# A two-layer decoder trunk on one core: gate loads issued before the end of the u loop, evened gathers, gate preparation in two pieces, the last tile of v in halves

## The chip, the core and the metric

The kernel runs on one core of a Trainium2 chip. The metric is the device time of one execution in microseconds (us), as the median of several runs. The core has a matrix engine (PE, with PEld for its weight loads), a vector engine (DVE), an activation engine (ACT), a general engine (POOL, which here issues indirect gathers) and a sequencer (SP, which here issues most loads). Each engine works through its own instructions in the order in which the program has them, and waits on semaphores for the others. DMA transfers are issued by SP, ACT or POOL into a queue of that engine and move the data on 16 DMA engines.

## The reference

A mixer (layer 1: gated linear attention, layer 2: stick-breaking attention, both with memory attention), a residual LayerNorm, a PEER expert layer and another LayerNorm, twice, over 512 tokens of width 1024. The change lies in PEER, which is computed once in each layer:

```
q = (xf @ w_q).reshape(N, PEER_HEADS, 2, PEER_QHALF)
s = jnp.einsum('nhpd,hpkd->nhpk', q, subkeys)
top_s, top_i = lax.top_k(s, PEER_TOPK)
cand_s = top_s[:, :, 0, :, None] + top_s[:, :, 1, None, :]
cand_i = top_i[:, :, 0, :, None] * PEER_KEYS + top_i[:, :, 1, None, :]
best_s, best_pos = lax.top_k(cand_s, PEER_TOPK)
idx = jnp.take_along_axis(cand_i, best_pos, axis=-1)
g = jax.nn.softmax(best_s, axis=-1)
act = jax.nn.gelu(jnp.einsum('nd,nhkd->nhk', xt, u_tab[it]), approximate=False)
return jnp.einsum('nhk,nhkd->nd', gt * act, v_tab[it])
```

Each token has 8 heads, and each head picks 16 of 16384 experts (128 x 128 pairs of keys): rows of two tables, u and v, with 16384 rows of 1024 floats. A token's output is the sum over its 128 experts of gate times gelu(u row . x) times v row.

## The kernel before

**Two ways for the tokens.** 384 of the 512 tokens (three token tiles of 128) take the dense way: the product of all 16384 u rows with the tokens on PE, a gelu, a multiplication with a dense matrix of gates that is zero where an expert wasn't picked, and the product with all 16384 v rows on PE. The first token tile, tile 0, takes the sparse way: POOL gathers its 128 rows per token of u, and then of v, from memory (L1103), and DVE multiplies and adds them up (L1156 for u, L1175 for v). The first 16 tokens of the dense tiles ("side" tokens) have their gelu through gathers as well, so that the u products are 368 tokens wide and the v weights 384. Each number is split into a high and a low half (`split`, L97 on ACT makes the high half, L98 on DVE the low one), and a product is three matmuls: high by high, high by low, low by high.

**The stages of `peer`.** First comes the query phase (17 rows). Then the u loop runs over 128 blocks of 128 experts: block b multiplies u's block (L117, L118, L119 into `ph`) and in the next iteration takes the gelu (L1626) of block b − 1. For blocks 0 to 111 it is written to memory (`Ad`); for the last 16 (`KEEP`) it stays in the tile `keep`. Beside that, small pieces of work are handed out by generators, a budget in ns per block: `lead` and `work` select the experts and prepare the gates of the three dense tiles, `gst` makes the dense gates from one-hot matrices (L1446 on PE, `ob` on DVE, `obl` on ACT) and writes them to memory (`Gd`, issued on ACT's queue, L1516), and `gus` issues the gathers and the work on them. `GU`, `GU2` and `GU3` are the budgets of the gathers, `GR` that of the gates, `VS` the first v block that hands out gather work, and `VE` the number of blocks that the rate `vb` keeps free at v's end.

**The v loop** runs over 128 blocks too, and starts with the 16 kept blocks. `vprep(i)` loads v's block (`vr`), loads the gates of a group of blocks (`gl`; the first 6 blocks' go to `g0`, a part of the tile of `keep`) and multiplies gates by activations into the weights `w` (L1700 on DVE for 368 columns, L1702 on ACT for the 16 side tokens), splits v (`vh`, `vl`) and w (`whi` L1704 on ACT, `wlo` L1705 on DVE). It runs two blocks ahead of the matmuls. Blocks 0 to 122 add into all three token tiles (L285, L287, L289 into `acc`), 18 matmuls a block. The last 5 (`TAIL`) are kept back and then multiplied token tile by token tile, 30 matmuls each, so that a tile's LayerNorm (L984 to L1001) runs while PE works on the next tile. The LayerNorm of tile 0 comes from the sum of the gathers (`va`) and ends the `gus` stream.

**What sets the order.** The u loop stands in a part of the program whose order a scheduler works out, and so do the first instructions of v on SP and POOL. The v loop is in a `manual_schedule` for DVE, ACT and PE: there each of them runs its instructions in the order in which the code emits them. SP's order is that of the loads as they are issued. `load_raw` has the raw tiles of u and v on SP's queue. `preload(1)` and `preload(2)` issue gate loads on ACT's queue.

## Time and profile before

| | us |
|---|---|
| median of 3 runs | 2862.17 |
| lowest, highest | 2860.47, 2863.76 |
| profiled execution | 2858.78 |
| its span in the trace | 2857.1 |
| v matmuls, idle before L285 | 4.5 |
| gathers on POOL, busy (u and v) | 392.8 and 311.8 |

A row of the costliest groups gives line, engine, operation, output and inputs, the count, the busy time, the mean of one in ns, and the idle time before with what ended it. Rows of a timeline give the start, the duration and, in brackets, the idle time before the instruction and what ended it; "SPq" and "ACTq" are the time that an engine's sequencer spent on issuing a DMA. Busy times of matmuls overlap, since they are pipelined; a window's row gives the merged busy time. The mean clock of PE over the span was 0.998 of full speed.

### The profile page before, as it was taken

What the parts mean: (1) busy time and instruction counts of PE and PEld (TensorE: products, weight loads), DVE (VectorE), ACT (ScalarE), POOL (GpSimd) and SP (SyncE); (2) the same over time, 40 slices, a digit from 0 to 9 for tenths busy, and PEclk for the clock granted to TensorE, in tenths of its full rate; (3) what the DMA queues carried; (4) which work ended last, traced back from release to release, by engine and by line L of the source; (5) the groups of instructions that cost most, each with busy time, mean ns of one, the idle gap of its engine ahead of it and who ended that gap; (6) DMA issues with size and microseconds to landing.
All of it is one profiled execution on the core that took longest, in us unless ns stands there. A gap on an engine that the chain in (4) does not pass through costs nothing. (4 is left out here: it accounts for less than half of the span.)

```text
span 2857.1 us, 44575 instructions
## 1 busy us (share of the span) xinstructions
PE 2829.1 (99%) x16144; PEld 2507.4 (88%) x16144; DVE 2410.4 (84%) x4944; ACT 1445.3 (51%) x2723; POOL 778.2 (27%) x584
## 2 busy tenths in 40 slices
PE   9999999999999999999999999999999999999998
PEld 7888899999998888888877789999999988888886
DVE  5567999999877888888868779999998778888888
ACT  6342446757674333433446424477676744334333
POOL 0100253333333333333000002433333333234330
PEclk9999999999999999999999999999999999999999
DMA  5332589989999999999521325989999999999994
GB/s 194 103 112 67 176 313 321 343 316 342 340 344 369 338 371 370 373 380 365 195 81 52 111 82 202 327 319 325 327 343 342 340 368 336 373 375 371 368 359 165
DMA packets 311070, 806.87 MB, mean 282 GB/s; under 512 B 32176, under 2 KB 124480, under 8 KB 304448
## 3 DMA queue, kind: packets, MB, share of 16 engines
q1 hardware_dynamic: 195936, 414.93, 42.0%
q0 software_dynamic: 78336, 285.25, 27.6%
q10 hardware_dynamic: 36576, 103.85, 9.5%
q8 instruction: 126, 2.06, 0.3%
q14 instruction: 96, 0.79, 0.1%
HBM read 708.19 MB, written 94.68 MB: 281 GB/s over the span
## 5 line engine op out<-in xcount | busy, mean ns | idle before, releaser
L117 PE MATMUL ph<-xhi,uh 128*128 128x368 f32 x2048 | 687.7, 336 | 0.0
L119 PE MATMUL ph<-xhi,ul 128*128 128x368 f32 x2048 | 674.0, 329 | 1.2 <-DVE ul L98 1.2
L118 PE MATMUL ph<-xlo,uh 128*128 128x368 f32 x2048 | 673.4, 329 | 0.0
L1103 POOL DMA_INDIRECT gr<-in_un,gidx x256 | 392.8, 1534 | 796.9 <-DVE gr L1156 595.3
L97 ACT ACTIVATE vh<-vr 128x1024 fp32r<-128x1024 f32 x256 | 271.3, 1060 | 497.7 <-PE acc L289 445.2
L1103 POOL DMA_INDIRECT gr<-in_vt,gidx x256 | 311.8, 1218 | 646.9 <-DVE va L1175 553.4
L285 PE MATMUL acc<-vh,whi 128*128 128x512 f32 x1536 | 474.5, 390 | 4.5 <-ACT whi L1704 4.5
L287 PE MATMUL acc<-vl,whi 128*128 128x512 f32 x1536 | 474.2, 390 | 0.2
L289 PE MATMUL acc<-vh,wlo 128*128 128x512 f32 x1536 | 473.6, 389 | 0.0
L98 DVE TENSOR_TENSOR vl<-vr,vh 128x1024 fp32r<-128x1024 f32 x256 | 313.5, 1225 | 160.1 <-ACT vh L97 156.6
L97 ACT ACTIVATE uh<-ur 128x1024 fp32r<-128x1024 f32 x288 | 304.1, 1056 | 197.9 <-PE ph L118 174.3
L119 PEld LDWEIGHTS ph<-xhi,ul 128*128 128x128 f32 x2048 | 384.7, 188 | 2.2 <-DVE ul L98 2.2
L118 PEld LDWEIGHTS ph<-xlo,uh 128*128 128x128 f32 x2048 | 385.4, 188 | 0.0
L117 PEld LDWEIGHTS ph<-xhi,uh 128*128 128x128 f32 x2048 | 385.1, 188 | 0.1
L98 DVE TENSOR_TENSOR ul<-ur,uh 128x1024 fp32r<-128x1024 f32 x288 | 351.1, 1220 | 34.3 <-ACT uh L97 34.3
L285 PEld LDWEIGHTS acc<-vh,whi 128*128 128x128 f32 x1536 | 287.9, 188 | 66.4 <-ACT whi L1704 7.0
L287 PEld LDWEIGHTS acc<-vl,whi 128*128 128x128 f32 x1536 | 288.3, 188 | 61.7 <-DVE vl L98 2.2
L289 PEld LDWEIGHTS acc<-vh,wlo 128*128 128x128 f32 x1536 | 288.2, 188 | 60.8 <-DVE wlo L1705 1.0
L1156 DVE SCALAR_TENSOR_TENSOR gr<-gr,xnat 128x1024 f32<-128x1024 f32 x256 | 310.3, 1218 | 24.5 <-DMA gr<-in_un,gidx 24.5
L1175 DVE SCALAR_TENSOR_TENSOR va<-gr,gw,va 128x1024 f32<-128x1024 f32 x254 | 325.2, 1281 | 1.0
L1491 ACT ACTIVATE obl<-ob,rat 128x128 f16<-128x128 f16 x736 | 234.1, 392 | 38.0 <-DVE ob L1468 18.3
L1704 ACT ACTIVATE whi<-w 128x384 fp32r<-128x384 f32 x256 | 131.1, 512 | 78.5 <-DVE w L1700 78.1
(358 smaller groups left out, 4091.4 us busy)
## 6 DMA issues: line engine op xcount, KB each, us to landing
ur<-in_ut SPq DMA_DIRECT2D x256, 512.0 KB
vr<-in_vt SPq DMA_DIRECT2D x256, 512.0 KB
Gd<-gt ACTq DMA_DIRECT2D x48, 1024.0 KB
Ad<-act ACTq DMA_DIRECT2D x112, 368.0 KB
al<-Ad SPq DMA_DIRECT2D x112, 368.0 KB
gl<-Gd SPq DMA_DIRECT2D x26, 1536.0 KB
ur<-in_wq SPq DMA_DIRECT2D x32, 512.0 KB
bs<-in_b_st SPq DMA_DIRECT2D x14, 512.0 KB
```

The lines of the kernel that those rows point to most:

```text
L97: nc.scalar.activation(hi, raw, AF.Copy)
L98: sub = lambda: eng.tensor_sub(lo, raw, hi.bitcast(F32))
L117: nc.tensor.matmul(ps, h, xhi[:, c, sl], start=(c == 0), stop=False)
L118: nc.tensor.matmul(ps, h, xlo[:, c, sl], start=False, stop=False)
L119: nc.tensor.matmul(ps, l, xhi[:, c, sl], start=False, stop=(c == NC - 1))
L285: nc.tensor.matmul(acc[hf], lh, hi[:, hf * 512:(hf + 1) * 512], start=first, stop=False)
L287: nc.tensor.matmul(acc[hf], lh, lo[:, hf * 512:(hf + 1) * 512], start=False, stop=False)
L289: nc.tensor.matmul(acc[hf], ll, hi[:, hf * 512:(hf + 1) * 512], start=False, stop=last)
L1103: nc.gpsimd.indirect_dma_start(out=gr, out_offset=None, in_=tab, in_offset=bass.IndirectOffsetOnAxis(ap=idx[:, k:k + 1], axis=0))
L1156: nc.vector.scalar_tensor_tensor(gr, gr, 1.0, xr, op0=ALU.mult, op1=ALU.mult, accum_out=dst[:, k:k + 1])
L1175: nc.vector.scalar_tensor_tensor(va, gr, gw[:, k:k + 1], va, op0=ALU.mult, op1=ALU.add)
L1491: nc.scalar.activation(obl[:, q], ob[:, q, 0], AF.Copy, scale=rat[:, n0 + q:n0 + q + 1])
```

## The change

Six edits go together. (1) `VS` goes from 3 to 6 and `VE` from 8 to 6, `GU2` from 1350 to 1420, `GU3` goes, and `GR2` = 1.6 is the gates' budget once `work` is empty: gathers and gates are handed out at other rates. (2) `gate_prep` yields after its first half. (3) The body of the u loop becomes the function `ublock`, which runs for blocks 0 to 117 as before; then the remaining `work` and `gst` are emptied, the pools of that stage are given back, and blocks 118 to 128 run at the head of v's hand-ordered part. (4) The first two gate loads are issued there, behind blocks 119 and 121, on SP's queue; the second goes to a new tile "vt". (5) That tile holds the high and low halves of v's last two blocks later. (6) The last token tile of the tail does one half of its columns for all five blocks, and then the other.

```
@@ -1034,16 +1034,17 @@
 GU = 1230
 LOG = 0
 PF = 3
-VS = 3
+VS = 6
 GD = 1
 G0 = 6
-VE = 8
-GU2 = 1350
-GU3 = 1900
+VE = 6
+GU2 = 1420
 WF = 6100
 ER = 6
 GQ = 900
 GR = 1.25
+GR2 = 1.6
+BX = 118
 LEAD = 3
 TAIL = 5
 RB = 4
@@ -1347,12 +1348,13 @@
                         nc.scalar.activation(iT.rearrange("p n k r -> p r k n")[:, k], pt[:, 0:2 * P].rearrange("p (k n) -> p k n", k=2), AF.Copy)
                         nc.vector.tensor_copy(gT[:, :, k], h16)
                     nc.vector.tensor_copy(ghi, h16)
+                    yield 1000
                     nc.vector.scalar_tensor_tensor(glo, gp_, GS, h16, op0=ALU.mult, op1=ALU.subtract)
                     nc.vector.tensor_scalar(rat, ghi, 1e-30, None, op0=ALU.max)
                     nc.vector.reciprocal(rat, rat)
                     nc.vector.tensor_mul(rat, rat, glo)
                     ready.append((self.t, rat, iT, gT))
-                    yield 2500
+                    yield 1900
 
                     if self.t * P == T0:
                         nc.vector.tensor_copy(siT, iT[:, :SD])
@@ -1608,7 +1610,10 @@
             gst = Stream(gates(list(range(SD, P, OT))), side_gates(), gates(2 * list(range(0, P, OT))))
             lead.c = -2000.0
             ab, ph, later = None, None, []
-            for b in range(P + 1):
+            big = keep = g0 = None
+
+            def ublock(b):
+                nonlocal ab, ph, big, keep, g0
                 if b == KB:
                     big = gp.tile([P, 16 * NT * P], F32, tag="big", name="keep")
                     keep = big[:, :KEEP * TU].rearrange("p (b n) -> p b n", n=TU)
@@ -1616,6 +1621,7 @@
                 if 0 < b <= KB:
                     if (b - 1) % AB == 0:
                         ab = wk.tile([P, AB, TU], F32, tag="act", name="act")
+                pn = None
                 if b < P:
                     if b > 0:
                         prep(b + 18, later)
@@ -1629,7 +1635,7 @@
                     if (b - 1) % AB == AB - 1:
                         nc.scalar.dma_start(Ad[(b - 1) // AB], ab)
                 ph = pn
-                gst(GR)
+                gst(GR if work.q else GR2)
                 while later:
                     later.pop(0)()
                 if lead.q:
@@ -1637,9 +1643,12 @@
                 else:
                     work(WB if ready else WB0)
                 if b < P - 1:
-                    gus(GU if work.q else GU2 if b < KB else GU3)
+                    gus(GU if work.q else GU2)
                 if LOG:
                     print("block", b, len(work.q), len(gst.q), len(gus.q), gcount)
+
+            for b in range(BX):
+                ublock(b)
             work.drain()
             gst.drain()
 
@@ -1652,7 +1661,6 @@
                     sl = slice(hf * 512, (hf + 1) * 512)
                     nc.sync.dma_start(out_dram[t * P:(t + 1) * P, sl], E.x[:, t, sl])
 
-        acc = [[psum(E, name=f"acc{t}_{h}") for h in range(2)] for t in range(ND)]
         vp = {}
 
         gcuts = [0, G0] + list(range(KEEP, P + 1, GB))
@@ -1664,12 +1672,16 @@
         def load_gates(eng, dst, b, b1):
             eng.dma_start(dst, Gd[:, :, b:b1].rearrange("s p i n -> p s i n"))
 
-        pre = {}
+        pre = {0: g0}
 
         def preload(k):
             i, i1 = gcuts[k:k + 2]
-            pre[i] = new_gates(i, i1)
-            load_gates(nc.scalar, pre[i], vorder[i], vorder[i] + i1 - i)
+            if k == 1:
+                pre[i] = wv.tile([P, 4 * D], F32, tag="vt", name="gl", bufs=1)[:, :NSUB * (i1 - i) * TS].rearrange(
+                    "p (s i n) -> p s i n", s=NSUB, n=TS)
+            elif k > 1:
+                pre[i] = new_gates(i, i1)
+            load_gates(nc.scalar if k > 1 else nc.sync, pre[i], vorder[i], vorder[i] + i1 - i)
 
         def vprep(i):
             if i >= P:
@@ -1678,10 +1690,7 @@
             raw = load_raw(E, vt[b * P:(b + 1) * P], "vr")
             if i in gcuts:
                 g1 = gcuts[gcuts.index(i) + 1]
-                if i == 0:
-                    vp["g"] = g0
-                    load_gates(nc.sync, g0, b, b + g1)
-                elif i in pre:
+                if i in pre:
                     vp["g"] = pre.pop(i)
                 else:
                     vp["g"] = new_gates(i, g1)
@@ -1700,18 +1709,24 @@
             nc.vector.tensor_mul(w[:, SD:].rearrange("p (s n) -> p s n", n=TS), vp["g"][:, SD // TS:, i - vp["i"]],
                                  av.rearrange("p (s n) -> p s n", n=TS))
             nc.scalar.activation(w[:, :SD].rearrange("p (s n) -> p s n", n=TS), vp["g"][:, :SD // TS, i - vp["i"]], AF.Copy)
-            hi, lo = split(E, raw, "v", wv if i >= P - (TAIL - 3) else None)
+            if i == P - (TAIL - 3):
+                vp["t"] = wv.tile([P, 4, D], F32R, tag="vt", name="vtail", bufs=1)
+                vp["n"] = iter(range(4))
+            hi, lo = split(E, raw, "v", (lambda name: vp["t"][:, next(vp["n"])]) if i >= P - (TAIL - 3) else None)
             nc.scalar.activation(whi, w, AF.Copy)
             nc.vector.tensor_sub(wlo, w, whi.bitcast(F32))
             vp[i] = (whi, wlo, hi, lo)
 
         tail = []
         with tc.manual_schedule(engines={mybir.EngineType.DVE, mybir.EngineType.Activation, mybir.EngineType.PE}):
+            for b in range(BX, P + 1):
+                ublock(b)
+                if b in (BX + 1, BX + 3):
+                    preload((b - BX) // 2)
+            acc = [[psum(E, name=f"acc{t}_{h}") for h in range(2)] for t in range(ND)]
             vb = 1200 * (2 * P + SD - gcount[0] + PF) / (P - VE - VS)
             vprep(0)
             vprep(1)
-
-            preload(1)
             for b in range(P):
                 vprep(b + 2)
                 if b == 1:
@@ -1743,8 +1758,16 @@
         with tc.manual_schedule(engines={eng.PE} if last else {eng.PE, eng.DVE}):
             for t in range(ND):
                 sl = slice(t * P, (t + 1) * P)
-                for k, (whi, wlo, hi, lo) in enumerate(tail):
-                    mov_mm(E, acc[t], whi[:, sl], wlo[:, sl], hi, lo, False, k == TAIL - 1)
+                if t < ND - 1:
+                    for k, (whi, wlo, hi, lo) in enumerate(tail):
+                        mov_mm(E, acc[t], whi[:, sl], wlo[:, sl], hi, lo, False, k == TAIL - 1)
+                else:
+                    for hf in range(2):
+                        hs = slice(hf * 512, (hf + 1) * 512)
+                        for k, (whi, wlo, hi, lo) in enumerate(tail):
+                            nc.tensor.matmul(acc[t][hf], whi[:, sl], hi[:, hs], start=False, stop=False)
+                            nc.tensor.matmul(acc[t][hf], whi[:, sl], lo[:, hs], start=False, stop=False)
+                            nc.tensor.matmul(acc[t][hf], wlo[:, sl], hi[:, hs], start=False, stop=k == TAIL - 1)
                 if last:
                     finish(t + 1, acc[t])
                 elif t < ND - 1:
```

In the lists that follow, a row is one instruction or a run of equal ones ("x4"), in the order of its engine, without times. Line numbers in the rows of the changed kernel are its own, up to 12 higher than before.

On DVE, the end of v in layer 0: `w`, `vl` and `wlo` are the three steps of one v block (vtail is vl of the last two), `lny` from `va` begins the LayerNorm of tile 0. Before, the part from the last use of the gathers:

```order
L1175 SCALAR_TENSOR_TENSOR va<-gr,gw,va 128x1024
L1700 TENSOR_TENSOR w<-gl,al 128x368
L98 TENSOR_TENSOR vl<-vr,vh 128x1024
L1705 TENSOR_TENSOR wlo<-w,whi 128x384
L984 SCALAR_TENSOR_TENSOR lny<-xnat,va 128x512
L985 BN_STATS lnst<-lny 128x6
```

That wlo is block 119's. After the LayerNorm's last row (L1001), w, vl and wlo follow eight times, for blocks 120 to 127. In the changed kernel, from that last row on:

```order
L1001 SCALAR_TENSOR_TENSOR xnat<-lny,lnsm,bet 128x512 x2
L1709 TENSOR_TENSOR w<-gl,al 128x368
L98 TENSOR_TENSOR vl<-vr,vh 128x1024
L1717 TENSOR_TENSOR wlo<-w,whi 128x384
L1709 TENSOR_TENSOR w<-gl,al 128x368
L98 TENSOR_TENSOR vtail<-vr,vtail 128x1024
L1717 TENSOR_TENSOR wlo<-w,whi 128x384
L1709 TENSOR_TENSOR w<-gl,al 128x368
L98 TENSOR_TENSOR vtail<-vr,vtail 128x1024
L1717 TENSOR_TENSOR wlo<-w,whi 128x384
L984 SCALAR_TENSOR_TENSOR lny<-xnat,acc_0_10222 128x512
```

The LayerNorm of tile 0 has moved from behind block 119 to behind block 124: three blocks (125 to 127) follow it, and then the LayerNorm of the tail's first tile.

On ACT, the turn from u to v in layer 0: `uh` is the high half of u's block 127, `keep<-ph` a gelu, `w<-keep`, `vh` and `whi` the three steps of one v block. Before:

```order
L97 ACTIVATE uh<-ur 128x1024
L1626 ACTIVATE keep<-ph 128x368
L1702 ACTIVATE w<-keep 128x16
L1626 ACTIVATE keep<-ph 128x368
L97 ACTIVATE vh<-vr 128x1024
L1704 ACTIVATE whi<-w 128x384
L1702 ACTIVATE w<-keep 128x16
L97 ACTIVATE vh<-vr 128x1024
L1626 ACTIVATE keep<-ph 128x368
L1704 ACTIVATE whi<-w 128x384
L1665 DMA gl<-Gd 128x24x160
L1626 ACTIVATE keep<-ph 128x368
```

In the changed kernel:

```order
L97 ACTIVATE uh<-ur 128x1024
L1632 ACTIVATE keep<-ph 128x368 x4
L1711 ACTIVATE w<-keep 128x16
L97 ACTIVATE vh<-vr 128x1024
L1716 ACTIVATE whi<-w 128x384
L1711 ACTIVATE w<-keep 128x16
```

The four gelus stand together ahead of v's first block, and the gate load is no longer on ACT at this place.

On SP, the loads from u's rows to v's first rows, layer 0: `keep<-Gd` is the load of the first gates, `gl<-Gd` a further one. Before:

```order
L82 DMA ur<-in_ut 128x1024 x77
L1665 DMA keep<-Gd 128x24x96
L82 DMA vr<-in_vt 128x1024 x4
L1695 DMA al<-Ad 128x736
L82 DMA vr<-in_vt 128x1024
```

In the changed kernel:

```order
L82 DMA ur<-in_ut 128x1024 x72
L1673 DMA keep<-Gd 128x24x96
L82 DMA ur<-in_ut 128x1024
L1673 DMA gl<-Gd 128x24x160
L82 DMA ur<-in_ut 128x1024 x4
L82 DMA vr<-in_vt 128x1024
L1704 DMA al<-Ad 128x736 x2
L82 DMA vr<-in_vt 128x1024
L1704 DMA al<-Ad 128x736
L82 DMA vr<-in_vt 128x1024 x2
L1673 DMA gl<-Gd 128x24x128
```

Two gate loads now have u rows behind them: five behind the first (blocks 123 to 127), four behind the second.

More of the change, by code (lines that the diff above doesn't have):

```diff
@@ L1036 @@
 PF = 3
-VS = 3
+VS = 6
 GD = 1
 G0 = 6
-VE = 8
-GU2 = 1350
-GU3 = 1900
+VE = 6
+GU2 = 1420
 WF = 6100
@@ L1046 @@
 GR = 1.25
+GR2 = 1.6
+BX = 118
 LEAD = 3
@@ L1349, in gate_prep @@
                     nc.vector.tensor_copy(ghi, h16)
+                    yield 1000
                     nc.vector.scalar_tensor_tensor(glo, gp_, GS, h16, op0=ALU.mult, op1=ALU.subtract)
@@ L1354, in gate_prep @@
                     ready.append((self.t, rat, iT, gT))
-                    yield 2500
+                    yield 1900
                     if self.t * P == T0:
@@ L1610, in peer, with ublock @@
             ab, ph, later = None, None, []
-            for b in range(P + 1):
+            big = keep = g0 = None
+            def ublock(b):
+                nonlocal ab, ph, big, keep, g0
                 if b == KB:
@@ L1618, in peer @@
                         ab = wk.tile([P, AB, TU], F32, tag="act", name="act")
+                pn = None
                 if b < P:
@@ L1631, in peer @@
                 ph = pn
-                gst(GR)
+                gst(GR if work.q else GR2)
                 while later:
@@ L1639, in peer @@
                 if b < P - 1:
-                    gus(GU if work.q else GU2 if b < KB else GU3)
+                    gus(GU if work.q else GU2)
                 if LOG:
                     print("block", b, len(work.q), len(gst.q), len(gus.q), gcount)
+            for b in range(BX):
+                ublock(b)
             work.drain()
@@ L1653, in finish @@
                     nc.sync.dma_start(out_dram[t * P:(t + 1) * P, sl], E.x[:, t, sl])
-        acc = [[psum(E, name=f"acc{t}_{h}") for h in range(2)] for t in range(ND)]
         vp = {}
@@ L1665, in load_gates @@
             eng.dma_start(dst, Gd[:, :, b:b1].rearrange("s p i n -> p s i n"))
-        pre = {}
+        pre = {0: g0}
         def preload(k):
             i, i1 = gcuts[k:k + 2]
-            pre[i] = new_gates(i, i1)
-            load_gates(nc.scalar, pre[i], vorder[i], vorder[i] + i1 - i)
+            if k == 1:
+                pre[i] = wv.tile([P, 4 * D], F32, tag="vt", name="gl", bufs=1)[:, :NSUB * (i1 - i) * TS].rearrange(
+                    "p (s i n) -> p s i n", s=NSUB, n=TS)
+            elif k > 1:
+                pre[i] = new_gates(i, i1)
+            load_gates(nc.scalar if k > 1 else nc.sync, pre[i], vorder[i], vorder[i] + i1 - i)
         def vprep(i):
@@ L1680, in vprep @@
                 g1 = gcuts[gcuts.index(i) + 1]
-                if i == 0:
-                    vp["g"] = g0
-                    load_gates(nc.sync, g0, b, b + g1)
-                elif i in pre:
+                if i in pre:
                     vp["g"] = pre.pop(i)
@@ L1702, in vprep @@
             nc.scalar.activation(w[:, :SD].rearrange("p (s n) -> p s n", n=TS), vp["g"][:, :SD // TS, i - vp["i"]], AF.Copy)
-            hi, lo = split(E, raw, "v", wv if i >= P - (TAIL - 3) else None)
+            if i == P - (TAIL - 3):
+                vp["t"] = wv.tile([P, 4, D], F32R, tag="vt", name="vtail", bufs=1)
+                vp["n"] = iter(range(4))
+            hi, lo = split(E, raw, "v", (lambda name: vp["t"][:, next(vp["n"])]) if i >= P - (TAIL - 3) else None)
             nc.scalar.activation(whi, w, AF.Copy)
@@ L1709, in peer @@
         with tc.manual_schedule(engines={mybir.EngineType.DVE, mybir.EngineType.Activation, mybir.EngineType.PE}):
+            for b in range(BX, P + 1):
+                ublock(b)
+                if b in (BX + 1, BX + 3):
+                    preload((b - BX) // 2)
+            acc = [[psum(E, name=f"acc{t}_{h}") for h in range(2)] for t in range(ND)]
             vb = 1200 * (2 * P + SD - gcount[0] + PF) / (P - VE - VS)
@@ L1712, in peer @@
             vprep(1)
-            preload(1)
             for b in range(P):
@@ L1745, in peer @@
                 sl = slice(t * P, (t + 1) * P)
-                for k, (whi, wlo, hi, lo) in enumerate(tail):
-                    mov_mm(E, acc[t], whi[:, sl], wlo[:, sl], hi, lo, False, k == TAIL - 1)
+                if t < ND - 1:
+                    for k, (whi, wlo, hi, lo) in enumerate(tail):
+                        mov_mm(E, acc[t], whi[:, sl], wlo[:, sl], hi, lo, False, k == TAIL - 1)
+                else:
+                    for hf in range(2):
+                        hs = slice(hf * 512, (hf + 1) * 512)
+                        for k, (whi, wlo, hi, lo) in enumerate(tail):
+                            nc.tensor.matmul(acc[t][hf], whi[:, sl], hi[:, hs], start=False, stop=False)
+                            nc.tensor.matmul(acc[t][hf], whi[:, sl], lo[:, hs], start=False, stop=False)
+                            nc.tensor.matmul(acc[t][hf], wlo[:, sl], hi[:, hs], start=False, stop=k == TAIL - 1)
                 if last:
```

## The prediction

> **What bounds the kernel now.** I began with the page's busy shares and costliest groups, then took the list of waits for what TensorE (PE) waits for, the windows for one stretch of each loop, and the timelines for the turn and for the end of v.
>
> ```profile
> PE 2829.1 (99%) x16144; PEld 2507.4 (88%) x16144; DVE 2410.4 (84%) x4944; ACT 1445.3 (51%) x2723; POOL 778.2 (27%) x584
> L285 PE MATMUL acc<-vh,whi 128*128 128x512 f32 x1536 | 474.5, 390 | 4.5 <-ACT whi L1704 4.5
> ```
> ```profile
> PE acc L285 <- ACT whi L1704: 4.5, 5, 2.5
> PE pg L1446 <- DVE ob L1438: 1.6, 2, 0.8
> PE ph L119 <- DVE ul L98: 1.2, 2, 0.6
> ```
> ```profile
> 855.00:876.00 21.00, 21.00 (x152) 20.43 (x152) 18.45 (x25) 14.02 (x34) 10.32 (x8) 1.00 0.99 375
> 926.00:1400.00 474.00, 474.00 (x2092) 392.48 (x2092) 407.18 (x493) 187.83 (x353) 151.57 (x123) 1.00 0.99 357
> ```
>
> PE is busy 99% of the span. The waits (total us, count, longest) say how little is left: 4.5 us for v's weights at the turns, 1.6 us for the gates' products, 1.2 us for u's low halves. The windows (us; busy of PE, weight loads, DVE, ACT, POOL; clock; DMA share; GB/s) show both loops full on PE at clock 1.00, with DVE at 88% and 86% (18.45/21, 407.18/474), and the DMA engines at a share of 0.99. So nothing inside the loops can become faster, with the matmul count unchanged; the change can win back only the waits at the turn and the gates, and it can lose wherever DVE, ACT or a load comes late. I cost it place by place, for both layers.
>
> **1. The end of v: a LayerNorm before three blocks instead of eight, loss.** VE goes from 8 to 6, so the gathers, and behind them tile 0's LayerNorm, end later: in DVE's order it now stands behind wlo of v block 124 (blocks count from 0; 123 to 127 are the tail), where before it stood behind wlo of block 119.
>
> ```profile
> 2804.33 0.69 DVE L984 SCALAR_TENSOR_TENSOR lny<-xnat,va 128x512 f32<-128x512 f32 x1
> ...
> 2810.90 0.53 DVE L1700 TENSOR_TENSOR w<-gl,al 128x368 f32<-128x368 f32 x1
> 2812.96 0.54 DVE L1700 TENSOR_TENSOR w<-gl,al 128x368 f32<-128x368 f32 x1
> ...
> 2824.26 0.55 DVE L1705 TENSOR_TENSOR wlo<-w,whi 128x384 fp32r<-128x384 f32 x1
> 2824.73 0.53 DVE L1700 TENSOR_TENSOR w<-gl,al 128x368 f32<-128x368 f32 x1
> ```
> ```profile
> 2811.53 0.53 ACT L1704 ACTIVATE whi<-w 128x384 fp32r<-128x384 f32 x1 [2.74 <-DVE w L1700]
> ...
> 2827.07 0.51 ACT L1704 ACTIVATE whi<-w 128x384 fp32r<-128x384 f32 x1
> ```
> ```profile
> 2828.62 0.62 PE L285 MATMUL acc<-vh,whi 128*128 128x512 f32 x2
> ...
> 2832.07 0.73 PE L285 MATMUL acc<-vh,whi 128*128 128x512 f32 x2 [0.34 <-ACT whi L1704]
> ```
>
> Timelines of layer 1 (start, duration). The LayerNorm held DVE from 2804.33 to 2810.90, 6.57 us, and DVE then caught up over eight blocks (w to w 2.06 us, 2810.90 to 2812.96, against 4.08 us that PE needs for a block by the window: 2092 matmuls in 474 us are 0.227 us each, 18 a block). Now wlo of block 124 still begins at 2824.26, since vl of 124 must wait for one of three buffers, which PE gives back after block 121. Behind it the LayerNorm runs first: w of block 125 begins at 2824.73 + 6.57 = 2831.30 instead of 2824.73. whi follows w after 0.63 us (2810.90 to 2811.53) and takes 0.51, so the tail's third group (block 125) starts on PE at about 2832.45 instead of 2828.62. Blocks 126 and 127 follow on DVE at 2.06 us each, so the tail's fifth group starts near 2832.45 + 4.12 = 2836.6 instead of 2832.07: **+4.55 us**. Everything after it in the tail is PE work with its operands ready, so the loss goes whole into the end. What stands ahead of the tail's LayerNorms cannot recover it. The idle of 3.8 us before block 125 may also lower the clock for a while; while PE is fed by DVE that costs little, and I take 0.5 us (bounds 0 and the 1.7 us of point 2). Two layers: 2 x 5.05 = **+10.1** (bounds 9.1 and 12.5).
>
> **2. The turn, gain.** Blocks 118 on now have their order written out: all gelus of u stand ahead of the first v block on ACT, where before w, vh and whi were mixed with them and with a gate load.
>
> ```profile
> 901.24 0.73 PE L285 MATMUL acc<-vh,whi 128*128 128x512 f32 x2 [0.37 <-ACT whi L1704]
> ...
> 919.17 0.73 PE L285 MATMUL acc<-vh,whi 128*128 128x512 f32 x2 [0.93 <-ACT whi L1704]
> ...
> 2322.32 0.88 PE L285 MATMUL acc<-vh,whi 128*128 128x512 f32 x2 [2.53 <-ACT whi L1704]
> ```
> ```profile
> 908.11 9.38 ACTq L1665 DMA_DIRECT2D gl<-Gd  x1
> 917.54 0.21 ACT L1702 ACTIVATE w<-keep 128x16 f32<-128x16 f32 x1 [8.65 <-issue]
> 917.66 1.04 ACT L97 ACTIVATE vh<-vr 128x1024 fp32r<-128x1024 f32 x1
> 918.61 0.51 ACT L1704 ACTIVATE whi<-w 128x384 fp32r<-128x384 f32 x1
> ...
> 2324.26 0.48 ACT L1626 ACTIVATE keep<-ph 128x368 f32<-128x368 f32 x1
> 2324.63 0.21 ACT L1702 ACTIVATE w<-keep 128x16 f32<-128x16 f32 x1
> ```
> ```profile
> 2319.50:2322.30 2.80, 0.29 (x2) 0.00 (x0) 2.33 (x4) 0.95 (x4) 0.82 (x1) 1.00 1.03 410
> 2322.70:2326.10 3.40, 3.40 (x10) 2.58 (x9) 3.35 (x7) 3.19 (x7) 0.00 (x0) 0.51 1.03 404
> ```
>
> PE idled 0.37 + 0.93 = 1.3 us at layer 0's turn (the second because ACT was held 9.38 us by issuing a gate load) and 2.53 us at layer 1's, after which the clock stood at 0.51 for 3.40 us: 1.7 us more. Now the last gelu waits for u's last matmul (0.37 us from 2324.26 to 2324.63), and then w, vh and whi of block 0 run: 917.54 to 919.17, 1.63 us until PE starts. With a tenth for the release that is 2.1 us idle in each layer. Layer 0: +0.8; layer 1: −0.4 and −1.7 for the clock. **−1.3** in all. If 2.1 us lowers the clock too, it is +1.7 in each layer, +2.1 in all; if it is wholly hidden, −5.5.
>
> [...]
>
> **3. Gate loads during u, loss.** Two gate loads now stand in SP's queue among the last ur loads, the second ahead of ur of blocks 124 to 127; before, SP had all ur ahead of its gate load, and the second went to ACT's queue after u.
>
> ```profile
> 903.08 0.38 ACTq L1665 DMA_DIRECT2D gl<-Gd  x1
> 921.95 0.21 ACT L1702 ACTIVATE w<-gl 128x16 f32<-128x16 f32 x1 [0.24 <-DMA gl<-Gd]
> ...
> 2296.40 0.33 ACTq L1516 DMA_DIRECT2D Gd<-gt  x1
> 2303.66 1.06 ACT L97 ACTIVATE uh<-ur 128x1024 fp32r<-128x1024 f32 x1 [2.58 <-PE ph L118]
> 2304.55 0.38 SPq L1665 DMA_DIRECT2D keep<-Gd  x1
> 2307.66 1.06 ACT L97 ACTIVATE uh<-ur 128x1024 fp32r<-128x1024 f32 x1 [2.58 <-PE ph L118]
> 2316.81 0.22 ACT L1702 ACTIVATE w<-keep 128x16 f32<-128x16 f32 x1 [7.73 <-DMA keep<-Gd]
> 2318.83 1.06 ACT L97 ACTIVATE vh<-vr 128x1024 fp32r<-128x1024 f32 x1 [1.44 <-DMA vr<-in_vt]
> ```
>
> SP waits at the first load until the last write of Gd has landed: 2296.40 to 2304.55, 8.15 us, with every ur behind it waiting too. The load itself landed 2316.81 − 2304.55 = 12.3 us after its issue, and a load behind it 14.3 us after (2318.83). The second is larger (128x24x160 instead of 128x24x96) and took 18.9 us at 903.08 to 921.95 on its own queue. After the last gate write near the start of block 116, that puts ur of block 124 at about 8.2 + 14.3 + 11 = 33 us, where 11 is my choice for the second load, overlapped with the first, between none and 18.9. A block of u lasts 4.0 us (uh at 2303.66 and 2307.66), and uh, 1.06 us, and ul must be made from the load first, some 2.5 us ahead of the block: 8 x 4.0 − 2.5 = 29.5 us is when it is needed. So PE stalls 0 to 5 us in each layer; I take 2, since the raw loads have two or three buffers in hand: **+4** (bounds 0 and 10). ACT's hold of 9.38 us goes, and w of block 6 no longer depends on it.
>
> **4. Gate preparation in two pieces, small gain.**
>
> ```profile
> 593.83 0.33 PE L119 MATMUL ph<-xhi,ul 128*128 128x368 f32 x1
> 594.95 0.23 PE L1446 MATMUL pg<-ob 128*128 128x128 bf16 x1 [0.80 <-DVE ob L1438]
> ```
>
> In DVE's order both pieces still run in one block, but the next tile's candidates move a block later and so behind the side gates' ob. This wait of 0.80 us, 1.2 with the restart, goes in each layer: **−2.4** (bounds 0 and −2.4). The other waits of that kind stay.
>
> **5. Last tile of v in halves, small gain.**
>
> ```profile
> 2845.49 1.41 DVE L1001 SCALAR_TENSOR_TENSOR xnat<-lny,lnsm,bet 128x512 f32<-128x512 f32 x2
> 2847.39 1.28 DVE L984 SCALAR_TENSOR_TENSOR lny<-xnat,acc 128x512 f32<-128x512 f32 x2 [0.48 <-PE acc L289]
> ```
>
> Tile 1's LayerNorm ends at 2846.90, and the last tile's lny, both halves, starts at 2847.39. With the first half finished 15 matmuls earlier, its lny runs before that, but the second half still waits for PE. I take the 0.48 us of waiting as the gain, in layer 1 alone: **−0.45** (bounds 0 and −0.6, half of the 1.28).
>
> **6. Taken at nothing:** the faster gate rate once the first stream is empty, the evened gathers and the two gathers that move into v. PE's 88% weight loads and full windows cover them, with DVE at 86 to 88%; a late ul would show as the 0.6 us of the third wait row, once or twice.
>
> **The sum:** 10.1 − 1.3 + 4 − 2.4 − 0.45 = +9.95. The profiled execution took 2858.78 us and so becomes 2868.7; the median of the runs lies 3.4 above it (2862.17), so I forecast **2872.1 us**.
>
> **Rivals.** (a) *The gate loads come in time*: ur has more buffers in hand than I allow, and point 3 costs nothing: 2868.1. For it: the loads' 8.2 + 14.3 alone is below 29.5. Against it: DMA share 0.99 and 18.9 us for such a load. (b) *The gate loads become the bound of the end of u and the turn dips*: 5 us in each layer instead of 2, and 1.7 of half clock twice: +9.4, 2881.5. (c) *Not slower*: the LayerNorm of tile 0 runs in DVE's slack before block 125 is wanted, since vl of 124 gets its buffer a block earlier than before. It decides from 4.55 us, a bit more than one block of 4.08: then point 1 falls away, 2862.0, and with point 3 in time as well 2858. Against it: vl of 124 stands ahead of the LayerNorm and PE sets when that buffer is free, and PE runs at the same pace. (d) *The change doesn't win its turn*: ACT still waits there for vr or g0, as 1.44 and 7.73 us above; with PE idle for 3 us instead of 2.1, about 2875, inside my range.
>
> **How the numbers follow.** Forecast 0.48 (with d), (a) 0.25, (b) 0.14, (c) 0.13. A run of this kernel can be told from no change by about 0.2%, 5.7 us: slower is above 2867.9, faster below 2856.4. The forecast and (b) are slower, (a) straddles the limit (0.13 slower, 0.12 same), (c) is same but for 0.04: slower 0.75, same 0.21, faster 0.04. The range runs from 2863, which leaves out most of (c), to 2882, which holds (b).
>
> **What would show it.** Right: on DVE, lny from xnat and va right behind wlo of block 124, and on PE an idle of nearly 4 us before the tail's third group, in both layers, with the wait for whi at over 10 us in all; at the turn one idle of about 2 us behind u's last matmul; PE waiting for uh or ul of block 124 on ur; one wait fewer for ob. Wrong: w of block 125 no later than before against PE's last block, or the gate loads landed with ur of 124 in hand, or a turn without idle.

## The result and the profile after

The changed kernel takes 2888.68 us (median of 4 runs, 2885.43 to 2890.34) against 2861.32 us before (4 runs beside it): a ratio of 1.0094, 95% interval 1.0076 to 1.0111. The change costs 27 us; the forecast was 10 us, with a range that ended at 2882. The profiled execution took 2888.77 us, 29.99 more than that of before.

First, as before, the page's busy shares and three of its costliest groups:

```profile
PE 2844.1 (99%) x16144; PEld 2520.0 (87%) x16144; DVE 2404.0 (83%) x4944; ACT 1449.0 (50%) x2723; POOL 857.8 (30%) x584
L117 PE MATMUL ph<-xhi,uh 128*128 128x368 f32 x2048 | 688.0, 336 | 5.4 <-ACT uh L97 5.4
L119 PE MATMUL ph<-xhi,ul 128*128 128x368 f32 x2048 | 675.4, 330 | 2.5 <-DVE ul L98 2.5
L285 PE MATMUL acc<-vh,whi 128*128 128x512 f32 x1500 | 465.5, 392 | 14.9 <-ACT whi L1716 14.9
```

PE is still busy 99% of the span, so the page alone hides 30 us. The idle columns show 10.4 us more before L285 and 5.4 us new before L117. That is 17 us with L119, and 30 us are to be found. PE's busy time is 15.0 us longer (2844.1 against 2829.1) for the same matmuls: the rest is in PE's clock. Windows (span, then busy of PE, weight loads, DVE, ACT, POOL; clock; DMA share; GB/s) around the places where the trace's clock records fall to half:

```profile
889.10:892.50 3.40, 3.40 (x13) 3.40 (x12) 3.40 (x6) 1.92 (x4) 2.67 (x2) 0.50 0.98 344
909.50:912.90 3.40, 3.40 (x10) 2.68 (x9) 3.40 (x5) 2.21 (x5) 0.00 (x0) 0.51 1.20 316
1418.20:1424.90 6.70, 5.91 (x14) 4.67 (x15) 5.84 (x9) 3.68 (x7) 0.00 (x0) 0.50 0.53 163
1452.30:1459.10 6.80, 6.44 (x28) 6.15 (x29) 2.38 (x4) 0.26 (x1) 0.00 (x0) 0.50 0.47 157
2322.70:2326.10 3.40, 3.13 (x10) 3.13 (x11) 3.40 (x6) 2.83 (x4) 1.68 (x1) 0.50 0.92 343
2343.20:2346.50 3.30, 3.30 (x8) 2.65 (x9) 3.30 (x6) 2.02 (x5) 0.00 (x0) 0.50 1.19 306
2623.10:2626.40 3.30, 3.30 (x9) 2.58 (x8) 3.30 (x5) 1.58 (x3) 1.00 (x1) 0.50 0.72 212
2858.60:2861.90 3.30, 3.28 (x8) 2.61 (x9) 3.30 (x6) 2.60 (x5) 0.00 (x0) 0.50 0.15 57
```

In each such stretch PE counts as busy, and does little more than half the work: matmuls of 368 columns that took 0.33 us take 0.51, and start 0.31 us apart instead of 0.17. There are eight of them before the last matmul, two of them 6.8 us long, against one of 3.4 us before: about 31 us more at half speed, a loss of up to 15 us that no idle column shows.

To place the loss, I took from both traces the start of the same matmul on PE (u block 80, the last of u, v block 16 and so on) and subtracted. The differences between neighbouring landmarks, in us, say where the time was lost:

| stretch | predicted, both layers | layer 0 | layer 1 |
|---|---|---|---|
| before u block 80 (gate preparation) | −2.4 | −1.00 | −1.06 |
| u block 80 to 122 (gates at the faster rate) | 0 | +0.82 | +0.76 |
| u block 122 to u's last matmul (gate loads) | +4 | +5.62 | +4.96 |
| u's last matmul to v block 16 (turn) | −1.3 | +1.65 | −0.13 |
| v block 16 to 120 | 0 | +0.72 | +5.73 |
| tail's start to v's last matmul | +10.1 | +5.67 | +4.49 |
| v's last matmul to the next u, or the end | −0.45 | +3.03 | −0.58 |

These add up to 30.7; 0.64 us less before the first u is the difference of two executions. Four stretches were far off: u's end, the turn, the middle of v, and the way from layer 0 into layer 1.

**u's end.** SP's and ACT's timelines of layer 0 (a row with x4 merges four issues and the time between them):

```profile
853.25 0.33 ACTq L1518 DMA_DIRECT2D Gd<-gt  x1
...
885.80 1.06 ACT L97 ACTIVATE uh<-ur 128x1024 fp32r<-128x1024 f32 x1 [7.40 <-DMA ur<-in_ut]
```
```profile
864.04 0.38 SPq L1673 DMA_DIRECT2D keep<-Gd  x1
864.51 5.34 SPq L82 DMA_DIRECT2D ur<-in_ut  x1
870.21 1.07 SPq L1673 DMA_DIRECT2D gl<-Gd  x1
871.38 10.17 SPq L82 DMA_DIRECT2D ur<-in_ut  x4
```
```profile
883.62 0.33 PE L119 MATMUL ph<-xhi,ul 128*128 128x368 f32 x1
886.91 0.44 PE L117 MATMUL ph<-xhi,uh 128*128 128x368 f32 x1 [2.95 <-ACT uh L97]
...
888.17 0.44 PE L119 MATMUL ph<-xhi,ul 128*128 128x368 f32 x1 [0.66 <-DVE ul L98]
```

The last gate write is issued at 853.25, SP's first gate load stands until 864.04, and ur of block 124 is there at 885.80, 32.6 us after the write (33 were worked out). PE idles 2.95 and 0.66 us, and then comes the half clock of 889.10.

**The turn** has the one idle that was forecast, behind the last gelu (ACT, then PE):

```profile
905.70 0.48 ACT L1632 ACTIVATE keep<-ph 128x368 f32<-128x368 f32 x1 [3.52 <-PE ph L119]
906.08 0.21 ACT L1711 ACTIVATE w<-keep 128x16 f32<-128x16 f32 x1
906.18 1.05 ACT L97 ACTIVATE vh<-vr 128x1024 fp32r<-128x1024 f32 x1
907.13 0.51 ACT L1716 ACTIVATE whi<-w 128x384 fp32r<-128x384 f32 x1
```
```profile
907.69 0.73 PE L285 MATMUL acc<-vh,whi 128*128 128x512 f32 x2 [2.03 <-ACT whi L1716]
```

It lasts 2.03 us (2.1 forecast), and half clock follows it in both layers (909.50 and 2343.20 above).

**The middle of v.** Behind block 64 of layer 1, ACT waits for LayerNorm's gamma, and then for vr (ACT's timeline, PE's below):

```profile
2616.57 0.20 ACT L1006 ACTIVATE junk<-gam 128x1 f32<-128x1 f32 x1 [6.09 <-DMA gam<-in_lng]
2616.68 0.20 ACT L1711 ACTIVATE w<-gl 128x16 f32<-128x16 f32 x1
2619.88 1.06 ACT L97 ACTIVATE vh<-vr 128x1024 fp32r<-128x1024 f32 x1 [3.00 <-DMA vr<-in_vt]
```
```profile
2621.40 0.73 PE L285 MATMUL acc<-vh,whi 128*128 128x512 f32 x2 [3.42 <-ACT whi L1716]
```

Over the whole kernel vh waits far more for vr than before (total us, count, longest; before, then after):

```profile
ACT vh L97 <- DMA vr<-in_vt: 52.5, 21, 5.9
ACT vh L97 <- DMA vr<-in_vt: 138.4, 50, 7.8
```

**The tail.** DVE and PE in layer 0: the LayerNorm of tile 0, then w of block 125, then PE's third group.

```profile
1411.21 0.69 DVE L984 SCALAR_TENSOR_TENSOR lny<-xnat,va 128x512 f32<-128x512 f32 x1
...
1417.79 0.54 DVE L1709 TENSOR_TENSOR w<-gl,al 128x368 f32<-128x368 f32 x1
```
```profile
1418.99 1.22 PE L285 MATMUL acc<-vh,whi 128*128 128x512 f32 x2 [3.72 <-ACT whi L1716]
```

That is the idle of point 1, to a tenth: 3.72 us (3.83 worked out). Behind layer 0's tail PE then waits for the last LayerNorm, and 1452.30 above is the half clock behind these two waits (before, the first was 0.52 us, and the clock stayed at 1.00):

```profile
1450.67 1.25 PE L966 MATMUL xtp<-ident,xnat 128*128 128x128 f32 x8 [1.57 <-DVE xlo L971]
1452.40 2.07 PE L133 MATMUL bsp<-xhi,bsl 128*128 128x256 f32 x8 [0.47 <-DVE bsl L98]
```

### The profile page after: what moved, and what is told of

It is laid out like the page before. It is cut to its first block, busy times and chain, and to the rows that moved or that the text cites. A ratio compares the mean times of both kernels' runs of the same rounds, so it can differ in the third digit from the quotient of the medians.

```text
span 2887.1 us, 44552 instructions
## 1 busy us (share of the span) xinstructions
PE 2844.1 (99%) x16144; PEld 2520.0 (87%) x16144; DVE 2404.0 (83%) x4944; ACT 1449.0 (50%) x2723; POOL 857.8 (30%) x584
## 3 DMA queue, kind: packets, MB, share of 16 engines
q8 instruction: 126, 2.06, 0.3%
## 5 line engine op out<-in xcount | busy, mean ns | idle before, releaser
L117 PE MATMUL ph<-xhi,uh 128*128 128x368 f32 x2048 | 688.0, 336 | 5.4 <-ACT uh L97 5.4
L119 PE MATMUL ph<-xhi,ul 128*128 128x368 f32 x2048 | 675.4, 330 | 2.5 <-DVE ul L98 2.5
L1104 POOL DMA_INDIRECT gr<-in_vt,gidx x256 | 392.1, 1532 | 530.7 <-DVE va L1176 474.0
L285 PE MATMUL acc<-vh,whi 128*128 128x512 f32 x1500 | 465.5, 392 | 14.9 <-ACT whi L1716 14.9
L287 PE MATMUL acc<-vl,whi 128*128 128x512 f32 x1500 | 464.8, 391 | 0.5
L289 PE MATMUL acc<-vh,wlo 128*128 128x512 f32 x1500 | 464.4, 391 | 0.0
L117 PEld LDWEIGHTS ph<-xhi,uh 128*128 128x128 f32 x2048 | 386.3, 189 | 6.1 <-ACT uh L97 6.0
L119 PEld LDWEIGHTS ph<-xhi,ul 128*128 128x128 f32 x2048 | 385.8, 188 | 3.7 <-DVE ul L98 3.7
L285 PEld LDWEIGHTS acc<-vh,whi 128*128 128x128 f32 x1500 | 282.7, 189 | 75.5 <-ACT whi L1716 17.1
```

The source lines that it names most:

```text
L117: nc.tensor.matmul(ps, h, xhi[:, c, sl], start=(c == 0), stop=False)
L119: nc.tensor.matmul(ps, l, xhi[:, c, sl], start=False, stop=(c == NC - 1))
L285: nc.tensor.matmul(acc[hf], lh, hi[:, hf * 512:(hf + 1) * 512], start=first, stop=False)
L287: nc.tensor.matmul(acc[hf], lh, lo[:, hf * 512:(hf + 1) * 512], start=False, stop=False)
L289: nc.tensor.matmul(acc[hf], ll, hi[:, hf * 512:(hf + 1) * 512], start=False, stop=last)
L1104: nc.gpsimd.indirect_dma_start(out=gr, out_offset=None, in_=tab, in_offset=bass.IndirectOffsetOnAxis(ap=idx[:, k:k + 1], axis=0))
```

## The experiments

Each run's profile was cut by the same landmarks; differences are against the profiled execution of before unless the text says otherwise. The times of the kernel before beside these runs were 2860.46 to 2861.91 us.

### The place of tile 0's LayerNorm (e1, e6)

e1 changes two constants of the changed kernel, e6 one of the kernel before:

```
e1: -VS = 6   +VS = 3        e6: -VE = 8   +VE = 3
    -VE = 6   +VE = 8
```

> The changed kernel with VE = 8 and VS = 3 as before, all else kept: five v blocks instead of three follow the LayerNorm of tile 0 on DVE. Theory (the LayerNorm ahead of blocks 125 to 127 makes the end of v late): w of block 125 comes at most 1 us too late, so the tail loses about 1 us a layer instead of 5.7 and 4.5, and the 3 us that layer 0's LayerNorms lose behind it go too; about 11 us less than the changed kernel. Rival (the halves of the last tile or PE's lower clock lose the time): both losses stay within 1 us.

> The kernel before with VE = 3 alone, so that three v blocks follow the LayerNorm of tile 0 on DVE, as in the changed kernel, while the gathers are less dense (one per 1.07 of a block's work instead of 1.12). Theory (the place of that LayerNorm makes the end of v late): +5 us between the tail's start and v's end in each layer, and 2 to 3 us more behind it in layer 0; +12 to +13 us in all, no idle in the middle of v. Rival (another part of the change): below 3 us.

e1 took 2869.39 us, 19.3 less than the changed kernel (about 11 expected). Its tails lose 0.29 and 0.33 us instead of 5.67 and 4.49. Behind layer 0's tail it still loses 1.64, not nothing, but the middle of v is on time in both layers, which the expectation did not have. e6 took 2869.09 us, 8.6 more than the kernel before (12 to 13 expected): the kernel before with that LayerNorm three blocks from the end loses 4.97 and 4.70 us in its tails, on the wait of PE's timeline that the changed kernel has:

```profile
2837.93 0.94 PE L285 MATMUL acc<-vh,whi 128*128 128x512 f32 x2 [3.71 <-ACT whi L1704]
```

Behind the tail of layer 0 it loses nothing (−0.18), where 2 to 3 us were expected. So the place of the LayerNorm makes the tails late, 9.5 us when it is taken back (e1) and 9.7 us when it is put in alone (e6), and it alone doesn't make the 3.0 us behind layer 0's tail.

### The gate loads (e2, e3)

In both, SP's loads of the blocks from 118 on are put in written order too. This takes a `manual_schedule` block of its own for the last u blocks, and as a side effect the order on ACT at the turn is no longer that of the changed kernel: in e2, w of block 0 comes ahead of the last four gelus, and vh and whi ahead of the last two.

```
+with tc.manual_schedule(engines=hand | {SP}):
     for b in range(BX, P + 1):
         ublock(b)
-        if b in (BX + 1, BX + 3):
-            preload((b - BX) // 2)
+        if b == BX + 1:          # e3 alone
+            preload(0)           # e3 alone
+    preload(0)                   # e2 alone
+    preload(1)
+with tc.manual_schedule(engines=hand):
```

> The changed kernel with both gate loads issued behind all of u's loads on SP, all else kept. Theory (u's blocks 123 and 124 wait for the gate loads ahead of them in SP's queue): PE's idle of 3 us and its half clock near block 124 go, 5 us less in each layer between blocks 122 and 127, but g0 lands near the end of u, so the turn may wait 0 to 3 us more. Rival (u's end is slow since DMA is full at that place): the idle stays at 2 us or more.

> The changed kernel with only the second gate load (blocks 6 to 15) issued behind all of u's loads, the first staying ahead of ur of blocks 122 to 127. If the second load is what makes u late: no idle of PE near block 124, 5 us less in each layer. If it is SP's wait for the last gate write at the first load: the idle stays at 2 to 3 us in each layer.

e2 took 2871.81 us. Its u's end loses −0.09 us in both layers: the stall and its half clock are gone, 10.8 us for the two layers. Its turn is 2.3 and 4.0 us faster than before, with no idle that the timeline shows, and not 0 to 3 us slower as I had feared for g0. e3 took 2877.60 us and loses 0.59 and 0.95 at u's end, and in layer 1 some 0.95 more just ahead of block 122: most of the stall came from the second load, less from SP's wait at the first. But e3 pays at layer 0's turn, where vr stands behind the second load (PE's timeline):

```profile
904.67 0.74 PE L285 MATMUL acc<-vh,whi 128*128 128x512 f32 x2 [3.44 <-ACT whi L1716]
```

### Idle or clock (e5)

Eight matmuls without a use fill PE's wait at the turn of the changed kernel:

```
+fill = psum(E, name="fill")
+for k in range(8):
+    nc.tensor.matmul(fill, E.xhi[:, 0, :P], E.xhi[:, 0], start=True, stop=True)
 acc = [[psum(E, name=f"acc{t}_{h}") for h in range(2)] for t in range(ND)]
```

> The changed kernel with eight extra matmuls (128x512, result not used) on PE between u's last matmul and v's first, 1.8 us of work in the 2.0 us in which PE idles there. Theory (it is the idle that lowers PE's clock, and the lowered clock costs 1.7 us beyond it): v's first matmul starts where it did, the half clock behind both turns goes, and v block 16 comes 1.7 us earlier against u's end in each layer. Rival (the clock falls there for another reason): the half clock stays, and nothing is gained.

PE's timeline and a window of e5, layer 0:

```profile
906.06 2.02 PE L1729 MATMUL fill<-xhi 128*128 128x512 f32 x8
908.26 0.73 PE L285 MATMUL acc<-vh,whi 128*128 128x512 f32 x2 [0.17 <-ACT whi L1717]
```
```profile
908.30:912.00 3.70, 3.58 (x15) 2.55 (x16) 3.70 (x7) 2.54 (x5) 0.00 (x0) 1.00 1.15 308
```

v's first matmul starts no earlier than in the changed kernel (+1.66 us from u's last matmul in both), the clock stays at 1.00, and from there to v block 16 e5 gains 1.59 us while the changed kernel has −0.01; in layer 1 it is −1.18 against +0.37. So a turn at half clock costs 1.55 to 1.6 us beyond the idle itself. (The whole run took 2882.32 us.)

That the idle is what lowers the clock, layer 0 of e5 does not show. e4 and e13 (below) have the changed kernel's turn without the eight matmuls; they too idle 2.03 us in layer 0, their clock stays at 1.00, and from v's first matmul to block 16 they gain as much as e5. In e13:

```profile
908.65 0.73 PE L285 MATMUL acc<-vh,whi 128*128 128x512 f32 x2 [2.03 <-ACT whi L1716]
```
```profile
908.70:912.10 3.40, 3.29 (x13) 2.33 (x14) 3.40 (x6) 2.54 (x5) 0.00 (x0) 1.00 1.16 311
```

Layer 1 speaks for it: there the idle lowered the clock in the changed kernel, e4 and e13, and with PE filled e5 didn't pay for it (−1.18 us against +0.37 above). That is one turn of one execution, and in e1 the unfilled idle of layer 1, 2.03 us too, left the clock at 1.00 as well; the last section has all these idles together.

### The middle of v (e4, e9, e10, e11, e13)

```
e4:  changed kernel  -warm_sqrt(E, vp["ln"][0])  +warm_sqrt(E, E.x[:, 0])
e13: changed kernel  -VS = 6   +VS = 3
e9:  e8 (below)      -VS = 3   +VS = 6
e10: e8 (below)      -VE = 8   +VE = 11
e11: e8 (below)      -VE = 8   +VE = 9, and the halves only in the last layer
```

> The changed kernel; at v block 64 ACT's table load no longer waits for the load of the LayerNorm's gamma (it reads a tile that is long there). Theory (ACT is held some 6 us by that wait, and behind it vh, whi and the next vr are late): the idle of 3.6 us with its half clock behind block 64 in layer 1 goes, 5.7 us less there and 0.7 less in layer 0. Rival (vr and the gathers are late there because DMA is full): at least 3 us of the loss stay.

e4 took 2889.13 us. The wait for gamma is gone, and with it the idle behind block 64; but in the blocks behind it layer 1 idles three times, at 2682, 2717 and 2751 us, about 34 us apart, as the gate loads of eight blocks (32.6 us of PE) and the idle itself make it, and the middle of v loses 6.46 us where the changed kernel lost 5.73. The hold of ACT was where a late v showed, not what made it late.

> The repaired kernel (e8) with VS = 6 instead of 3: gather work starts at v block 6 and is denser, 1400 ns a block instead of 1364, over 114 blocks. If starting late is what leaves the middle of v short of loads (vr late, PE idle at the groups of gates): idle of PE there again, 2 to 7 us in the two layers, and 6 us less margin everywhere else. If density alone decides: the same as in e10. If neither: no idle in the middle of v, as in e8.

> The repaired kernel (e8) with VE = 11 instead of 8: gather work starts at v block 3 and is as dense as in e9, 1400 ns a block over 114 blocks, with eight blocks behind the LayerNorm of tile 0. If density is what makes the middle of v late: PE idles there, 2 to 7 us, as in e9. If the late start does it: no idle there, and the 0.3 us that each tail of e8 still loses go, 0.6 us less than e8.

> The repaired kernel (e8) with VE = 9 and the halves in the last layer alone. Theory: the 0.8 us that layer 0 loses behind its tail go (the halves cost 1.0 there by e7), and 0.3 to 0.6 of the tails; about 1.2 us less than e8, 6 us less than the kernel before, ratio 0.998. Rival: no difference from e8 that can be told.

> The changed kernel with VS = 3 alone: gather work in v is spread over 119 blocks instead of 116, 1341 ns a block instead of 1376, and the LayerNorm of tile 0 stays where the change put it. If density decides the idle in the middle of v: none there in either layer, 6.4 us less than the changed kernel, and all its other losses (u's end, turn, tails) stay. If the late end of u or the late LayerNorm made it: at least 2 us of it stay.

The rate `vb` at which gather work is handed out in v is 1200 ns times the gather steps left (133 in the changed kernel, 131 before) over the blocks that carry them. Ordered by it, loss between v blocks 16 and 120 in us, and how long vh waited for vr in the whole kernel:

| run | ns a block | VS | layer 0 | layer 1 | vh on vr |
|---|---|---|---|---|---|
| e6 | 1289 | 3 | 0 | 0 | 78.5 |
| e13 | 1341 | 3 | 0.37 | 0.77 | 120.7 |
| e15 | 1341 | 1 | 0 | 0 | 62.8 |
| before | 1344 | 3 | 0 | 0 | 52.5 |
| e7 | 1344 | 3 | 0 | 0 | 56.4 |
| e12 | 1344 | 3 | 0.51 | 0.17 | 113.3 |
| e1 | 1364 | 3 | 0 | 0 | 76.3 |
| e8 | 1364 | 3 | 0 | 0 | 77.8 |
| e14 | 1364 | 3 | 0 | 0.33 | 105.6 |
| changed kernel | 1376 | 6 | 0.72 | 5.73 | 138.4 |
| e11 | 1376 | 3 | 0 | 10.04 | 156.2 |
| e9 | 1400 | 6 | 2.91 | 1.53 | 145.3 |
| e10 | 1400 | 3 | 7.06 | 11.06 | 170.2 |

e2 to e5, all at 1376 with VS = 6, lose 7.0, 5.9, 6.5 and 4.6 us. So nine executions at 1364 ns a block or less lose at most 1.1 us, and eight at 1376 or more lose 4.4 to 18.1: the border lies within 1%. With the same late tail and the same late end of u, e13 loses 1.1 us where the changed kernel loses 6.5, by VS alone, which sets both the rate and the start (2881.92 us in all; no loss was expected). e9 and e10 have one rate and two starts, and both lose (4.4 us as expected, and 18.1 where 2 to 7 were): a late start isn't needed for the loss. e9 took 2859.80 us and e10 2872.64. How much is lost at one rate scatters. e11's profiled execution, at 2862.95 us, is the slowest of its ten; their median is 2.9 us above that of e14, which differs from e11 in VE alone. One row of the waits of e10, beside that of the changed kernel above:

```profile
ACT vh L97 <- DMA vr<-in_vt: 170.2, 52, 8.1
```

The DMA share in v was about 1 already before (0.96 to 1.04 in windows of 50 to 210 us). That a denser hand-out of gathers makes vr late is what the table shows, the waits more loosely than the losses (e12 has 113.3 us of them at the old rate). How it does so stays open. SP can issue a load of vr only when DVE's vl has given a buffer back, and it waits for that in the changed kernel as before (layer 1, 2400 to 2810 us; before 172.2 us in 70 waits):

```profile
SPq L82 <- DVE vl L98: 146.4, 65, 6.7
```

So slower transfers and buffers that come back later from DVE would both fit, and no run separates them.

### The halves and the gate preparation alone (e7, e12)

The two edits of the diff, each alone in the kernel before.

> The kernel before with the last token tile in halves alone. Theory: 0.5 us less behind PE's last matmul in layer 1, and in layer 0 nothing or up to 1 us more at the start of the next mixer, since DVE's LayerNorm chain and not PE ends last there; the 3 us lost there in the changed kernel then come from the late LayerNorms instead. Rival: the halves cost 2 us or more in layer 0.

> The kernel before with the gate preparation in two pieces alone. Theory: the second of the two waits for ob in each layer goes, 1.0 to 1.2 us less before u block 80 in each layer, nothing elsewhere; 2.1 us in all. Rival (the shift comes from the other gate rate): nothing changes before block 80.

e7 took 2862.93 us: 0.65 us less at the end, 1.00 more behind layer 0's tail, where PE waits 1.10 us for xlo of DVE's last LayerNorm, against 0.52 before. Other executions bear this out: with the halves in both layers and tile 0's LayerNorm no later than before, 0.80 to 1.64 us are lost there (e1, e8, e9, e10); without them in layer 0, nothing (e6, e12, e14, e15), but 0.54 in e11. e12 took 2857.76 us: −1.00 and −1.06 us before u block 80, nothing else in u, as expected. Each of these figures is of one execution, and places that the edit doesn't touch differ too: from u's last matmul to v block 16 by +2.1 and +1.0 us in e7 and by −0.8 in e12's layer 1, and by +1.1 at e12's end.

### The repaired kernel (e8, e14, e15)

e8 is e1 and e2 together; e14 is e8 with the halves only in the last layer (`if t < ND - 1 or not last:`); e15 is e14 with VS = 1.

> The changed kernel with VE = 8 and VS = 3 and with both gate loads behind all of u's loads (the two repairs together; the second also lets w and vh of block 0 run between the last gelus). Theory (the parts add up: 12.8 us over the kernel before with the gate loads late, less about 11 for the LayerNorm's place and 4 to 7 for the middle of v): 2 to 6 us faster than the kernel before, ratio 0.998 to 0.9995. Rival (the middle of v stays late, since the loads there are late anyway): 2 us or more slower than before.

> The repaired kernel (e8, 1364 ns a block) with the halves in the last layer alone. If 1376 ns a block made e11 idle in the middle of v: none here, and 0.8 us less than e8 behind layer 0's tail; 5 to 6 us less than the kernel before. If e11's idle came from the halves: it comes here too, 3 us or more.

> As e14 with VS = 1: 1341 ns a block. If more distance from 1376 helps: as e14 or up to 1 us less, with less spread between runs. Rival (gather work beside the first v blocks disturbs them): 0.5 us or more lost up to v block 16 in each layer.

| run | median, us | ratio to before | 95% interval |
|---|---|---|---|
| e8 | 2855.39 | 0.9983 | 0.9974 to 0.9993 |
| e11 | 2857.56 | 0.9986 | 0.9976 to 0.9995 |
| e14 | 2854.64 | 0.9974 | 0.9964 to 0.9984 |
| e15 | 2853.82 | 0.9974 | 0.9965 to 0.9984 |

All four beat the kernel before, by 0.1 to 0.3%, e14 and e15 by 7 to 8 us; among the four the intervals overlap. e11 was expected 1.2 us below e8 and came 2.2 above it. e14 lost 0.33 us in the middle of v and nothing behind layer 0's tail, as expected, but 1.87 in layer 1's tail, which no run explains. e15's runs lie no closer together than those of e14. The change had gains in it: 2.1 us from the gate preparation, 2.0 and 1.7 us in layer 0's turn and 3.1 and 3.7 in layer 1's (e8 and e15, u's last matmul to v block 16; −1.0 to −2.6 and −2.0 to −3.7 in the six executions of e8 to e11, e14 and e15, against +0.4 to +2.1 and −1.2 to +1.0 in e6, e7 and e12), 0.6 us from the halves in the last layer. e8's turn in layer 0, from ACT and PE: two gelus now stand behind vh of block 0, and PE goes from u (its last matmul at 900.37) to v without a wait.

```profile
899.11 1.06 ACT L97 ACTIVATE vh<-vr 128x1024 fp32r<-128x1024 f32 x1 [5.90 <-DMA vr<-in_vt]
900.08 0.51 ACT L1716 ACTIVATE whi<-w 128x384 fp32r<-128x384 f32 x1
...
902.64 0.46 ACT L1632 ACTIVATE keep<-ph 128x368 f32<-128x368 f32 x1
```
```profile
900.37 0.33 PE L119 MATMUL ph<-xhi,ul 128*128 128x368 f32 x1
900.64 0.73 PE L285 MATMUL acc<-vh,whi 128*128 128x512 f32 x2
```

## Why the prediction was wrong

The direction and the largest term were right; the size was 17 us short, and the range with it. By the profiled executions it was 20 us short (30.0 against 9.95): the forecast had added 3.4 us from the profile to the median, and the changed kernel's median is that of its profile. Step by step:

1. **End of v: right.** +10.1 forecast, +10.16 measured; e1 and e6 show the mechanism from both sides. That the sum fits so closely is luck: the two layers lost 5.67 and 4.49, with a half clock of 6.8 us in one and 3.4 in the other, and the same late tails lost 4.48 to 5.67 in other runs. Rival (c), that DVE has slack enough there, is refuted by e6.
2. **Turn: the mechanism right, the size wrong.** "2.1 us idle in each layer" was 2.03. I let that idle cost nothing in clock, a choice of mine that no run had shown, though the text names the case ("if 2.1 us lowers the clock too, it is +1.7 in each layer, +2.1 in all"): it did, in both layers, and they sum to +1.5. e5 shows what the clock cost; e1, e4 and e13 each paid it in one layer only, so that both layers paid it here is in part chance.
3. **Gate loads: the mechanism right, the size wrong.** My own numbers gave 33 us against a need at 29.5, so 3.5 us; I then took 2 "since the raw loads have two or three buffers in hand". PE idled 2.95 + 0.66 in layer 0. And the half clock behind it was in no part of this term: +10.6 instead of +4, just past the upper bound of 10. e2 and e3 show that the second load made most of it. Rival (b) priced this place at 10 us and the half clock at both turns, and came nearest (2881.5); what it lacks is the middle of v and the way into layer 1. The turn of (d) didn't come: PE waited there for the gelu's chain, not for vr or g0.
4. **Gate preparation: right.** −2.4 forecast, −2.06 measured, alone in e12.
5. **Halves: half right.** −0.58 at the end (−0.45 forecast). That layer 0 would lose by them was not seen: PE there runs into the next mixer, and it then waits for DVE's last LayerNorm, 1.00 us in e7. In the changed kernel the wait comes with the late LayerNorms and a half clock of 6.8 us, +3.03.
6. **"Taken at nothing … PE's 88% weight loads and full windows cover them": this step failed.** The two gathers moved into v and the new VS and VE make gather work 2.4% denser, and I asked whether PE and DVE had room for it on average, and not whether the loads of vr would still come in time. The row quoted for that very window has a DMA share of 0.99. The middle of v lost 6.45 us, and e13 takes 5.3 of them back by VS alone; whether the transfers or DVE's buffers made vr late stays open. The stretch with the faster gate rate cost 1.6 us more, which e8, too, still pays (+1.15 and +0.74). The gathers' budgets GU2 and GU3 change there as well, and no run separates them.

Half clock stood behind all four places that were far off (u's end, the turns, layer 1's middle of v, the way into layer 1). By the row at 2322.70 that I had quoted, each idle of 2 us or more ought to have had up to 1.7 us in its bounds: 3.4 at u's ends and 3.4 at the turns.

## What to carry to other kernels

On a full PE give an idle of 2 us or more a possible loss at half clock on top (1.55 to 1.6 us behind 2.03 us here, paid at some turns and not at others), and look for that loss in the clock column, since PE counts as busy there. Where a loop runs at a DMA share of 1, don't ask only whether the engines have room for a moved gather: 1% more of them per block stood here between 1 us at most and 4 us or more. A wait that ends last where a loop is late (gamma in the middle of v) need not be its cause: take it away, and see whether the loss moves.
